# Causal attention on one core: row maxima of heads 1 to 7 sent through DRAM, and the maxima's mask added by a matmul

## The chip, the cores and the metric

The kernel runs on one core of a Trainium2 chip. A core has five engines that run their own queues of instructions and wait for each other by semaphores: TensorE (PE; its weight loads are shown apart as PEld), VectorE (DVE), ScalarE (ACT), GpSimd (POOL) and SyncE (SP), which here does nothing but issue DMAs. Matrix products land in PSUM, eight banks of 128 x 512 float32; other tiles lie in SBUF. The metric is the time of one execution on the device, in microseconds (us).

## What is computed

One layer of a decoder trunk: an input projection, an mLSTM branch of 4 heads, an attention branch of 8 heads, an output projection and an MLP. The change lies in the attention:

```python
SEQ, MLA_HEADS, MLA_NOPE, MLA_ROPE, MLA_V = 2048, 8, 64, 32, 64
scale = (MLA_NOPE + MLA_ROPE) ** -0.5
sc = jnp.einsum('bhqd,bkhd->bhqk', q, k) * scale
sc = jnp.where(kpos[None, :] <= qpos[:, None], sc, -jnp.inf)
p = jax.nn.softmax(sc, axis=-1)
h = jnp.einsum('bhqk,bkhd->bqhd', p, v)
```

## The kernel before

The program is a list of small operations, each with an engine, an estimated duration, the operations it needs, a key (a due time) and the buffers of a ring that it takes and frees. `Plan.run` (line 154) simulates the engines with these estimates and lays the operations down in the order that comes out; `pin` (line 255) then holds each engine but SP to that order. So estimates, such as `n / 2.4 + 15` ns for a matmul of `n` columns, decide which instruction stands behind which, and an engine never runs its queue in another order. SP's DMAs stand in the planned order too.

Attention goes head by head (h = 0 to 7) and in each head over four blocks of 512 queries (qb = 0 to 3). For a pair (h, qb) there are two stages:

- *Maxima* (`maxima`, line 1548). For each of four groups j of 128 queries and each block kb <= qb of 512 keys, one matmul (line 1569) makes rough scores in one of three PSUM banks (rings "m" and "q"), and VectorE reduces them to one maximum per query in `mp`. Where kb < qb this is a plain reduction (line 1574). Where kb = qb, the diagonal piece of (j + 1) x 128 columns, a custom instruction adds the causal mask `maskneg` and takes the maximum in one go, followed by a read of the accumulator (line 1576). There are 192 plain and 128 diagonal pieces in all. Then `top_` (line 1595) reduces `mp` to `mx`, 128 partitions by 4; `rows_` (line 1600) turns that into one row of 512 by four matmuls against the identity, into a bank of the same rings, called `mt`; and `put` (line 1603) copies the row, negated, into partition 96 of the query tile `QK`. The key tile has ones there, so the score matmuls subtract each query's maximum on their own.
- *Steps* (`step`, line 1615). For each tile kt of 128 keys, three matmuls of split float32 operands make transposed scores S (lines 245 to 247); on the diagonal a fourth, in bf16, adds the mask (line 1629: `identb` as weights, `maskb` streamed, 128 columns). ScalarE takes the exponential twice (lines 1633 and 1637), VectorE or GpSimd the low part pl (line 1641), and PE multiplies with V (lines 1652 to 1657). At a block's end ScalarE and VectorE take the product out (ot, lines 1724 and 1727; ou, line 1731), SP stores it, and the sums go through DRAM (sumd, rsm, recd; lines 1738 to 1748).

The maxima are planned to run ahead of the steps that need them (`LEAD`, some 25 tiles). A score of (h, qb) needs the row of (h, qb).

Of the kernel before, what the change touches and what calls it, by code (L numbers as in the profile page):

```python
# [22 lines left out]
TB = 512  # L23
# [4 lines left out]
NH = 8  # L28
QSCALE2 = 96.0
NEG = -3.0e38  # L30
# [7 lines left out]
TB_ = 1  # L38
TR_ = 1
EARLY = ()  # L40
EKEY = -165.0
EGAP = 1.5
LOL = 20.0
# [60 lines left out]

C_CONVW, C_CONVB, C_GPRE, C_HN, C_QN, C_KVN, C_N = 0, 16, 20, 28, 32, 34, 35

K_ID, K_MASKT, K_INV, K_OFF, K_NOT, K_C, K_MASK, K_N = 0, 128, 256, 257, 258, 259, 259, 771

R_BG, R_POST, R_PRE, R_POSTM, R_N = 0, 8, 8 + DM, 8 + 2 * DM, 8 + 3 * DM

# [10 lines left out]
def f32(ap):  # L121
    return ap.bitcast(F32)


class Plan:
# [11 lines left out]
    def ring(self, name, bufs, when=None):  # L137

        self.rings[name] = [bufs, [], when]
# [97 lines left out]
def trunk(ctx: ExitStack, tc: tile.TileContext, x, xT, pos, wu, wout, wup, wdn, cols, rows, consts, edge, out, dbg=None):  # L237
# [3 lines left out]
    vec, act, pool, pe = nc.vector, nc.scalar, nc.gpsimd, nc.tensor  # L241
    dma = nc.sync.dma_start
# [6 lines left out]
    def sb(stack, name, bufs, side="left"):  # L249
        return stack.enter_context(tc.tile_pool(name=name, bufs=bufs, side=side, reuse_waits="tile"))  # L250
# [35 lines left out]
    trep = [dram.tile([P, 2, TB], F32, tag=f"trep{b}", name=f"trep{b}") for b in range(NB)]  # L286
    trigd = dram.tile([64, SEQ], F32, tag="trigd", name="trigd")
    sumd = dram.tile([NH, SEQ], F32, tag="sumd", name="sumd")
    recd = dram.tile([NH, SEQ], F32, tag="recd", name="recd")
    x1d = out  # L290
    x1Td = dram.tile([DM, SEQ // 2], F32, tag="x1Td", name="x1Td")
# [4 lines left out]
    pl = Plan()  # L296
# [1107 lines left out]

    V = {}
    pools = {}
    a2 = av = ar2 = pq = pS = po = onecol = maskneg = maskb = identb = None
    pm = []
    QK, Qh, Ql, Kh, Kl = ([None, None] for _ in range(5))

# [5 lines left out]

    def switch1():

        nonlocal a2, maskneg, pq
        s_e.close()  # L1420
        a2 = sb(pc, "a2", 2)
        a1 = sb(pc, "a1", 1)
        set_tiles(a1, 0)
        maskneg = a1.tile([P, 512], F32, tag="maskneg", name="maskneg")
        pq = pp(pc, "pq", 1)

    def switch2():
# [4 lines left out]

    def switch3():

        nonlocal av, ar2, pS, po, maskb, identb, onecol
        s_b.close()
        pools["work0"] = sb(ctx, "work0", 1, "right")
        av = sb(pa, "av", 1, "right")
        maskb = av.tile([P, P], BF16, tag="maskb", name="maskb")
        identb = av.tile([P, P], BF16, tag="identb", name="identb")  # L1440
        act.copy(maskb, maskT)
        act.copy(identb, ident)
# [70 lines left out]
    o_kr, o_k, o_q, o_m, o_sc, o_pv, o_v = {}, {}, {}, {}, {}, {}, {}  # L1513
# [34 lines left out]
    def maxima(h, qb, keys):  # L1548
        s = h % 2
        mp = {}  # L1550
        reds = []

        def ring(i):
            return "q" if (h, qb) in EARLY or i % 3 == 2 else "m"

        def bank(i, name):
            return (pq if ring(i) == "q" else pm[0]).tile([P, TB], F32, tag=ring(i), name=name)

        def piece(j, kb, key):
            n = TB if kb < qb else (j + 1) * P  # L1560
            t = {}
            i = len(reds)

            def mm():
                if "t" not in mp:
                    mp["t"] = a2.tile([P, 4, 4], F32, tag="mp", name=f"mp{h}_{qb}", bufs=4)
                q0 = qb * TB + j * P
                t["p"] = ps = bank(i, f"m{h}_{qb}_{j}_{kb}")
                pe.matmul(ps[:, :n], Qh[s][0:96, q0 : q0 + P], Kh[s][0:96, kb * TB : kb * TB + n], start=True, stop=True)  # L1569

            def red():
                ps = t["p"]
                if kb < qb:
                    vec.tensor_reduce(mp["t"][:, j, kb : kb + 1], ps, axis=AX.X, op=ALU.max)  # L1574
                else:
                    vec.tensor_tensor_reduce(  # L1576
                        out=ps[:, :n], in0=ps[:, :n], in1=maskneg[:, 512 - n :], op0=ALU.add, op1=ALU.max, scale=1.0, scalar=NEG,
                        accum_out=mp["t"][:, j, kb : kb + 1],
                    )

            head = not reds
            a = pl.op("PE", n / 2.4 + (56 if n == P else 15), mm, [o_q[h, qb][0], o_k[h, kb][0], o_kr[s, kb], o_const[s]], key, take=(ring(i), "mp") if head else (ring(i),))
            if head:
                mp["op"] = a
            reds.append(pl.op("DVE", n / 0.96 + (148 if kb < qb else 285), red, [a, o_mask] if head else [a, o_mask, mp["op"]], key - 3, free=[(ring(i), a)]))

        todo = [(j, kb) for j in range(4) for kb in range(qb + 1)]
        for (j, kb), key in zip(todo, keys):
            piece(j, kb, key)
        t = {}  # L1590
        key = keys[-1] - 3

        def top_():
            t["m"] = a2.tile([P, 32], F32R, tag="mx", name=f"mx{h}_{qb}")[:, 0:4]
            vec.tensor_reduce(t["m"], mp["t"][:, :, 0 : qb + 1], axis=AX.X, op=ALU.max)

        def rows_():
            t["p"] = bank(len(reds), f"mt{h}_{qb}")
            for j in range(4):
                pe.matmul(t["p"][0:1, j * P : (j + 1) * P], t["m"][:, j : j + 1], identr, start=True, stop=True)  # L1600

        def put():
            act.activation(Qh[s][96:97, qb * TB : (qb + 1) * TB], t["p"][0:1], AF.Copy, scale=-1.0)
# [3 lines left out]
        war = [o_sc[n] for n, (hh, q, _) in enumerate(blocks) if (hh, q) == (h - 2, qb)]  # L1607
# [195 lines left out]
    n = GT * P  # L1803
# [856 lines left out]
def prepare(inputs):  # L2660
    a = {k: np.asarray(v) for k, v in inputs.items()}
# [24 lines left out]
    def cv(v):  # L2686
# [7 lines left out]
    consts = np.zeros((P, K_N), np.float32)  # L2694
    consts[:, K_ID : K_ID + P] = np.eye(P)
    r = np.arange(P)
    consts[:, K_MASK + 384 : K_MASK + 512] = np.where(r[None, :] <= r[:, None], 0.0, NEG)
    consts[:, K_MASKT : K_MASKT + P] = np.where(r[None, :] >= r[:, None], 0.0, NEG)
# [39 lines left out]
```

## Time and profile before

| | us |
|---|---|
| time before, median of 3 runs | 2419.19 |
| the three runs | 2416.09, 2419.19, 2419.89 |
| the profiled execution, its own time | 2418.22 |
| its span in the profile | 2415.7 |
| PE busy in the span | 2372.5 |
| first matmul of the maxima, start | 516.0 |
| last step of attention on VectorE (line 1641), start | 992.1 |

The span is 2.5 us shorter than the execution's time; what lies around it is start and end. A row of the profile's timeline gives start, duration, engine, line of the kernel, operation, and output<-inputs with their shapes. PE's rows overlap, as a matmul's duration holds its way through the array; the time that one takes from the next is the distance of their starts. In the waits, "PEld S L245 <- DVE pl L1641" says that a weight load for S waited for VectorE's pl.

### The profile page before, as it was taken

Reading aid. Unit: us, or ns where it says so; the run is one execution under the profiler, and the core shown is the slowest. Engines: PE = TensorE matmul, PEld = TensorE weight load, DVE = VectorE, ACT = ScalarE, POOL = GpSimd, SP = SyncE. Lnnn points to the kernel's source line nnn. Section 1 sums busy time; section 2 is a strip of 40 time slices with the busy share of each in tenths; the row PEclk is TensorE's granted clock in tenths of the full one; section 3 lists DMA queues with packets and bytes.
Section 4 is the critical chain, followed back from the end, with each engine's and each line's share of the span. In section 5 each row is a group of like instructions: output and inputs, shape, how many; then the busy total and the mean of one; then the engine's idle time right before and its main releaser. Section 6 shows DMA issues by size and latency. Waiting matters only on the chain.

```text
span 2415.7 us, 34327 instructions
## 1 busy us (share of the span) xinstructions
PE 2372.5 (98%) x11135; PEld 1907.3 (79%) x11135; DVE 1722.8 (71%) x3125; ACT 1363.1 (56%) x2646; POOL 814.0 (34%) x697
## 2 busy tenths in 40 slices
PE   9999999999999999999999999999999999999997
PEld 7787777777777777788888888888888888888885
DVE  6865665658888887646866687766675677676778
ACT  5645454437788777544666556755665343443454
POOL 2634343428888888432000000000000322322346
PEclk9999999989999999999999999999999999999999
DMA  7697979887222321567877697755664435445448
GB/s 280 219 320 229 336 239 337 271 208 168 72 57 54 80 60 26 157 202 249 258 213 227 195 327 225 210 171 166 184 214 144 159 127 183 129 136 169 133 136 167
DMA packets 341308, 449.21 MB, mean 186 GB/s; under 512 B 34908, under 2 KB 227432, under 8 KB 341128
## 3 DMA queue, kind: packets, MB, share of 16 engines
q1 hardware_dynamic: 337192, 440.16, 58.6%
q0 software_dynamic: 3936, 6.87, 2.0%
q8 instruction: 87, 1.43, 0.2%
q14 instruction: 93, 0.76, 0.1%
HBM read 295.97 MB, written 153.05 MB: 186 GB/s over the span
## 4 chain that ended last, share of the span: by engine, by line
PE 53%; DVE 1%; DMA 1%; issue 0%; ACT 0%; SPq 0%; POOL 0%; DVEq 0%; ACTq 0%; POOLq 0%
PE op L245 1%; PE op L246 1%; PE op L247 1%; PE d_4X L2510 1%; PE d_3X L2512 1%; PE d_5X L2512 1%; PE d_4X L2512 1%; PE d_1X L2512 1%; PE d_1X L2511 1%; PE d_2X L2511 1%; PE d_3X L2511 1%; PE d_2X L2512 1%; PE d_4X L2511 1%; PE d_5X L2511 1%; PE d_5X L2510 1%; PE d_1X L2510 1%
## 5 line engine op out<-in xcount | busy, mean ns | idle before, releaser
L2548 POOL TENSOR_TENSOR y<-vd_0X,y 128x512 f32<-128x512 f32 x7 | 10.3, 1475 | 726.1 <-ACT vd_0X L2545 726.1
L1668 POOL TENSOR_TENSOR t<-t,ph 128x512 f32<-128x512 f32 (+1 forms) x192 | 213.0, 1110 | 17.8 <-ACT ph L1633 7.4
L1633 ACT ACTIVATE ph<-S 128x512 fp32r<-128x512 f32 (+1 forms) x320 | 170.4, 533 | 84.2 <-PE S L247 51.7
L2460 ACT CAST hh<-hr 128x512 fp32r<-128x512 f32 (+1 forms) x208 | 116.3, 567 | 156.1 <-DMA hr<-hd 15.3
L1641 DVE TENSOR_TENSOR pl<-S,ph 128x512 fp32r<-128x512 f32 (+3 forms) x272 | 157.1, 589 | 33.1 <-ACT S L1637 30.2
L245 PE MATMUL mm<-xh,wh 128*128 128x512 f32 x384 | 157.2, 409 | 5.4 <-ACT vs L813 1.9
L2465 DVE TENSOR_TENSOR hl<-hr,hh 128x512 fp32r<-128x512 f32 (+1 forms) x208 | 133.0, 647 | 30.2 <-ACT hh L2460 23.9
L246 PE MATMUL mm<-xl,wh 128*128 128x512 f32 x384 | 151.3, 394 | 0.9 <-DVE xl L416 0.9
L247 PE MATMUL mm<-xh,wl 128*128 128x512 f32 x384 | 151.1, 393 | 0.5 <-DVE wl L491 0.5
L1574 DVE TENSOR_REDUCE mp<-m 128x1 f32<-128x512 f32 x192 | 128.7, 681 | 19.1 <-PE m L1569 18.4
L1637 ACT ACTIVATE S<-S 128x512 f32<-128x512 f32 (+3 forms) x272 | 140.8, 518 | 0.4
L245 PE MATMUL S<-QK 97*128 97x512 f32 (+1 forms) x320 | 121.3, 379 | 2.4 <-DVE pl L1641 2.3
L1654 PE MATMUL o<-ph,V 128*128 128x512 f32 (+1 forms) x320 | 118.9, 378 | 2.2 <-DVE ot L1727 1.8
L1569 PE MATMUL m<-QK 96*128 96x512 f32 (+3 forms) x320 | 117.7, 400 | 1.3 <-DVE mp L1576 0.6
L246 PE MATMUL S<-QK 97*128 97x512 f32 (+1 forms) x320 | 118.2, 369 | 0.0
L247 PE MATMUL S<-QK 97*128 97x512 f32 (+1 forms) x320 | 117.8, 368 | 0.0
L1657 PE MATMUL o<-pl,V 128*65 128x512 f32 (+1 forms) x320 | 115.6, 362 | 0.6 <-POOL pl L1641 0.5
L245 PE MATMUL op<-wo,hh 128*128 128x512 f32 x256 | 101.0, 395 | 0.3 <-DVE osm L1958 0.2
L2299 ACT ACTIVATE t<-t 128x512 f32<-128x512 f32 x96 | 60.6, 632 | 70.8 <-DVE t L2294 70.1
L247 PE MATMUL op<-wo,hl 128*128 128x512 f32 x256 | 99.9, 390 | 0.0
L246 PE MATMUL op<-wo,hh 128*128 128x512 f32 x256 | 99.8, 390 | 0.0
L245 PEld LDWEIGHTS mm<-xh,wh 128*128 128x128 f32 x384 | 72.5, 189 | 26.9 <-ACT vs L813 2.4
(6451 smaller groups left out, 7485.9 us busy)
## 6 DMA issues: line engine op xcount, KB each, us to landing
hr<-hd SPq DMA_DIRECT2D x100, 448.0 KB
wr<-in_wu_dram SPq DMA_DIRECT2D x71, 512.0 KB
hd<-t SPq DMA_DIRECT2D x128, 256.0 KB
hd<-ts SPq DMA_DIRECT2D x96, 256.0 KB
wl<-wparts SPq DMA_DIRECT2D x45, 512.0 KB
QK<-qkd SPq DMA_DIRECT2D x32, 512.0 KB
xt<-in_x_dram SPq DMA_DIRECT2D x28, 512.0 KB
xf<-xd SPq DMA_DIRECT2D x40, 256.0 KB
```

The source lines that it names most:

```text
L245: pe.matmul(o, ah, bh, start=start, stop=False)
L246: pe.matmul(o, ah, bl, start=False, stop=False)
L247: pe.matmul(o, al, bh, start=False, stop=stop)
L1574: vec.tensor_reduce(mp["t"][:, j, kb : kb + 1], ps, axis=AX.X, op=ALU.max)
L1633: act.activation(t["h"][:, :w], t["S"][:, :w], AF.Exp)
L1637: act.activation(t["p"][:, :w], t["S"][:, :w], AF.Exp)
L1641: (pool if by_pool else vec).tensor_tensor(t["l"][:, :w], t["p"][:, :w], f32(t["h"][:, :w]), ALU.subtract)
L1654: pe.matmul(o0, v[:, 0:128], t["h"][:, :w], start=start, stop=stop)
L1668: pool.tensor_tensor(to, to, hv, ALU.add)
L2465: vec.tensor_tensor(t["l", m][:, :w], t["r", m][:, :w], f32(t["h", m][:, :w]), ALU.subtract)
L2511: pe.matmul(ps, a, w[:, 1], start=False, stop=False, skip_group_check=True)
L2512: pe.matmul(ps, b, w[:, 0], start=False, stop=stop, skip_group_check=True)
```

## The change

1. Diagonal pieces of the maxima: a bf16 matmul of 128 columns adds the mask in PSUM (weights `maskb`, streamed `identb`), and VectorE makes a plain reduction of n columns. The custom instruction, the accumulator read and the tile `maskneg` with its load are gone.
2. For heads 1 to 7 (`MROW = 1`), `rows_` and `put` are gone. SP writes `mx` to DRAM (`lay`, 512 elements of 4 bytes) and reads the row back into partition 96 of `QK` (`fetch`, 2 KB). Head 0 keeps the matmuls and the copy. `mx` has three buffers for two.
3. The sign moves: the key tile has -1 in partition 96, and the row isn't negated.
4. The bf16 mask and identity come ready from the host in the constants; ScalarE's two casts are gone.
5. The planner's estimates follow: 60 ns for the mask matmul, `n / 0.96 + 148` ns for the reduction.

```diff
-    maskT = cst[:, K_MASKT : K_MASKT + P]
+    maskb, identb = (cst[:, K_MASKT + i : K_MASKT + i + P // 2].bitcast(BF16) for i in (0, P // 2))
...
-        ("mp", 4, o_s1), ("mx", 2, o_s1), ("rsm", 2, o_s3),
+        ("mp", 4, o_s1), ("mx", 3, o_s1), ("rsm", 2, o_s3),
...
-    o_mask = pl.op("SP", 500, lambda: dma(maskneg, consts[:, K_MASK : K_MASK + 512]), [o_s1], key=EKEY - 30, kb=256)
...
-                pe.matmul(ps[:, :n], Qh[s][0:96, q0 : q0 + P], Kh[s][0:96, kb * TB : kb * TB + n], start=True, stop=True)
+                pe.matmul(ps[:, :n], Qh[s][0:96, q0 : q0 + P], Kh[s][0:96, kb * TB : kb * TB + n], start=True, stop=kb < qb)
+                if kb == qb:
+                    pe.matmul(ps[:, n - P : n], maskb, identb, start=False, stop=True)
...
-                ps = t["p"]
-                if kb < qb:
-                    vec.tensor_reduce(mp["t"][:, j, kb : kb + 1], ps, axis=AX.X, op=ALU.max)
-                else:
-                    vec.tensor_tensor_reduce(
-                        out=ps[:, :n], in0=ps[:, :n], in1=maskneg[:, 512 - n :], op0=ALU.add, op1=ALU.max, scale=1.0, scalar=NEG,
-                        accum_out=mp["t"][:, j, kb : kb + 1],
-                    )
+                vec.tensor_reduce(mp["t"][:, j, kb : kb + 1], t["p"][:, :n], axis=AX.X, op=ALU.max)
...
-            act.activation(Qh[s][96:97, qb * TB : (qb + 1) * TB], t["p"][0:1], AF.Copy, scale=-1.0)
+            act.activation(Qh[s][96:97, qb * TB : (qb + 1) * TB], t["p"][0:1], AF.Copy)
+
+        def lay():
+            dma(mrowd[h, qb * TB : (qb + 1) * TB].rearrange("(j p) -> p j", p=P), f32(t["m"]))
+
+        def fetch():
+            dma(f32(Qh[s][96:97, qb * TB : (qb + 1) * TB]), mrowd[h : h + 1, qb * TB : (qb + 1) * TB])
...
+        if h >= MROW:
+            b = pl.op("SP", 500, lay, [a], key, free=[("mx", a)], kb=128)
+            o_m[h, qb] = pl.op("SP", 500, fetch, [b] + war, key, kb=64)
+            return
...
-        "edge": np.stack([np.ones(SEQ, np.float32), np.zeros(SEQ, np.float32)]),
+        "edge": np.stack([-np.ones(SEQ, np.float32), np.zeros(SEQ, np.float32)]),
```

Lines of the changed kernel are numbered a little otherwise: 1565 for the maxima's matmul, 1567 for its mask, 1570 for the reduction, 1597 for `lay`, 1600 for `fetch`, 246 to 248 for the three matmuls.

The orders of the two programs agree but for attention. Three places are shown; a name such as m_1_0_1 is a piece of qb 1, j 0, kb 1.

PE in the first part, head 0, before the first scores. Before:

```order
L1600 MATMUL mt_0_5143<-identr,mx_0_5137 1x128 x4
L1569 MATMUL m_1_0_1_5149<-QK_4840 128x128
L1569 MATMUL m_1_1_1_5156<-QK_4840 128x256
L1569 MATMUL m_1_2_0_5165<-QK_4840 128x512
L1569 MATMUL m_1_2_1_5168<-QK_4840 128x384
L1569 MATMUL m_1_3_0_5171<-QK_4840 128x512
```

And now:

```order
L1591 MATMUL mt_0_5145<-identr,mx_0_5140 1x128 x4
L1565 MATMUL m_1_0_1_5151<-QK_4841 128x128
L1567 LDWEIGHTS cst
L1567 MATMUL m_1_0_1_5151<-cst 128x128
L1565 MATMUL m_1_2_1_5157<-QK_4841 128x384
L1567 LDWEIGHTS cst
L1567 MATMUL m_1_2_1_5157<-cst 128x128
L1565 MATMUL m_1_1_1_5161<-QK_4841 128x256
L1567 LDWEIGHTS cst
L1567 MATMUL m_1_1_1_5161<-cst 128x128
L1565 MATMUL m_1_2_0_5174<-QK_4841 128x512
```

Each diagonal piece is followed by its mask, a weight load and a matmul of 128 columns, and the diagonal pieces have moved ahead of the wide ones. The set mt stays, as this is head 0.

PE in the steady part, head 4, block 2 of the steps, where the row of block 3 is made. Before:

```order
L247 MATMUL S_2_5_8621<-QK_4840 128x512
L1600 MATMUL mt_3_8629<-identr,mx_3_8617 1x128 x4
L1654 MATMUL o_4_2_8585<-ph_2_11_8576,V_5246 128x128
L1657 MATMUL o_4_2_8586<-pl_2_11_8594,V_5246 65x128
L1569 MATMUL m_0_3_0_8641<-QK_5248 128x512
```

And now:

```order
L248 MATMUL S_2_5_8640<-QK_4841 128x512
L1565 MATMUL m_0_1_0_8652<-QK_5257 128x256
L1567 LDWEIGHTS cst
L1567 MATMUL m_0_1_0_8652<-cst 128x128
L1565 MATMUL m_0_3_0_8655<-QK_5257 128x512
L1567 LDWEIGHTS cst
L1567 MATMUL m_0_3_0_8655<-cst 128x128
L1655 MATMUL o_4_2_8602<-ph_2_11_8591,V_5255 128x128
L1658 MATMUL o_4_2_8603<-pl_2_11_8610,V_5255 65x128
```

The set mt is gone from its place, and two masks of the next head's maxima stand there.

SP at the same place. Before:

```order
L1738 DMA sumd<-ou_1_8563 1x512
L1748 DMA recd<-rsm_0_8533 128x4
L1737 DMA hT<-ot_1_8560 64x512
L1742 DMA rsm_1_8664<-sumd 128x4
L1748 DMA recd<-rsm_1_8664 128x4
```

And now:

```order
L1739 DMA sumd<-ou_1_8584 1x512
L1749 DMA recd<-rsm_0_8545 128x4
L1738 DMA hT<-ot_1_8572 64x512
L1743 DMA rsm_1_8681<-sumd 128x4
L1597 DMA mrowd<-mx_3_8645 128x4x1
L1600 DMA QK_4841<-mrowd 1x512
L1597 DMA mrowd<-mx_0_8700 128x4x1
L1600 DMA QK_5257<-mrowd 1x512
L1749 DMA recd<-rsm_1_8681 128x4
```

Two lays and two fetches stand between the load and the store of rsm_1, behind the store of ot_1.

More of the change, by code (lines that the diff above doesn't have):

```diff
@@ L40 @@
 EARLY = ()
+MROW = 1
 EKEY = -165.0
@@ L1406, in trunk @@
     pools = {}
-    a2 = av = ar2 = pq = pS = po = onecol = maskneg = maskb = identb = None
+    a2 = av = ar2 = pq = pS = po = onecol = None
     pm = []
@@ L1417, in switch1 @@
     def switch1():
-        nonlocal a2, maskneg, pq
+        nonlocal a2, pq
         s_e.close()
@@ L1423, in switch1 @@
         set_tiles(a1, 0)
-        maskneg = a1.tile([P, 512], F32, tag="maskneg", name="maskneg")
         pq = pp(pc, "pq", 1)
@@ L1433, in switch3 @@
     def switch3():
-        nonlocal av, ar2, pS, po, maskb, identb, onecol
+        nonlocal av, ar2, pS, po, onecol
         s_b.close()
@@ L1438, in switch3 @@
         av = sb(pa, "av", 1, "right")
[L1439 to L1442, printed above, removed]
         ar2 = sb(pa, "ar2", 2, "right")
@@ L1568, in mm @@
                 t["p"] = ps = bank(i, f"m{h}_{qb}_{j}_{kb}")
-                pe.matmul(ps[:, :n], Qh[s][0:96, q0 : q0 + P], Kh[s][0:96, kb * TB : kb * TB + n], start=True, stop=True)
+                pe.matmul(ps[:, :n], Qh[s][0:96, q0 : q0 + P], Kh[s][0:96, kb * TB : kb * TB + n], start=True, stop=kb < qb)
+                if kb == qb:
+                    pe.matmul(ps[:, n - P : n], maskb, identb, start=False, stop=True)
             def red():
-                ps = t["p"]
-                if kb < qb:
-                    vec.tensor_reduce(mp["t"][:, j, kb : kb + 1], ps, axis=AX.X, op=ALU.max)
-                else:
-                    vec.tensor_tensor_reduce(
-                        out=ps[:, :n], in0=ps[:, :n], in1=maskneg[:, 512 - n :], op0=ALU.add, op1=ALU.max, scale=1.0, scalar=NEG,
-                        accum_out=mp["t"][:, j, kb : kb + 1],
-                    )
+                vec.tensor_reduce(mp["t"][:, j, kb : kb + 1], t["p"][:, :n], axis=AX.X, op=ALU.max)
             head = not reds
-            a = pl.op("PE", n / 2.4 + (56 if n == P else 15), mm, [o_q[h, qb][0], o_k[h, kb][0], o_kr[s, kb], o_const[s]], key, take=(ring(i), "mp") if head else (ring(i),))
+            a = pl.op("PE", n / 2.4 + (56 if n == P else 15) + (60 if kb == qb else 0), mm, [o_q[h, qb][0], o_k[h, kb][0], o_kr[s, kb], o_const[s]], key, take=(ring(i), "mp") if head else (ring(i),))
             if head:
                 mp["op"] = a
-            reds.append(pl.op("DVE", n / 0.96 + (148 if kb < qb else 285), red, [a, o_mask] if head else [a, o_mask, mp["op"]], key - 3, free=[(ring(i), a)]))
+            reds.append(pl.op("DVE", n / 0.96 + 148, red, [a] if head else [a, mp["op"]], key - 3, free=[(ring(i), a)]))
         todo = [(j, kb) for j in range(4) for kb in range(qb + 1)]
@@ L1602, in put @@
         def put():
-            act.activation(Qh[s][96:97, qb * TB : (qb + 1) * TB], t["p"][0:1], AF.Copy, scale=-1.0)
-        a = pl.op("DVE", 80, top_, reds, key, take=("mx",), free=[("mp", mp["op"])])
+            act.activation(Qh[s][96:97, qb * TB : (qb + 1) * TB], t["p"][0:1], AF.Copy)
[3 more added lines that the diff above has]
+            dma(f32(Qh[s][96:97, qb * TB : (qb + 1) * TB]), mrowd[h : h + 1, qb * TB : (qb + 1) * TB])
+        a = pl.op("DVE", 80, top_, reds, key, take=("mx",), free=[("mp", mp["op"])])
+        war = [o_sc[n] for n, (hh, q, _) in enumerate(blocks) if (hh, q) == (h - 2, qb)]
+        if h >= MROW:
+            b = pl.op("SP", 500, lay, [a], key, free=[("mx", a)], kb=128)
+            o_m[h, qb] = pl.op("SP", 500, fetch, [b] + war, key, kb=64)
+            return
         b = pl.op("PE", 4 * 75, rows_, [a, o_const[s]], key, take=(ring(len(reds)),), free=[("mx", a)])
-        war = [o_sc[n] for n, (hh, q, _) in enumerate(blocks) if (hh, q) == (h - 2, qb)]
         o_m[h, qb] = pl.op("Activation", 585, put, [b] + war, key, free=[(ring(len(reds)), b)])
@@ L2693, in prepare @@
     rows = np.concatenate([a["b_gates"][0], a["norm_post_mix"][0], a["norm_pre_mlp"][0], a["norm_post_mlp"][0]])[None]
-    consts = np.zeros((P, K_N), np.float32)
+    consts = np.zeros((P, K_C), np.float32)
     consts[:, K_ID : K_ID + P] = np.eye(P)
     r = np.arange(P)
-    consts[:, K_MASK + 384 : K_MASK + 512] = np.where(r[None, :] <= r[:, None], 0.0, NEG)
-    consts[:, K_MASKT : K_MASKT + P] = np.where(r[None, :] >= r[:, None], 0.0, NEG)
+    halves = np.concatenate([np.where(r[None, :] >= r[:, None], 0.0, NEG), np.eye(P)], axis=1).astype(np.float32)
+    consts[:, K_MASKT : K_MASKT + P] = np.ascontiguousarray((halves.view(np.uint32) >> 16).astype(np.uint16)).view(np.float32)
     inv = np.array(INV_FREQ_BITS, np.uint32).view(np.float32)
```

5 lines of the change are left out of this document (3 added, 2 removed).

## Prediction

> **What bounds the kernel now.** I read the page first: the engines' busy time and the chain that ended last.
>
> ```profile
> PE 2372.5 (98%) x11135; PEld 1907.3 (79%) x11135; DVE 1722.8 (71%) x3125; ACT 1363.1 (56%) x2646; POOL 814.0 (34%) x697
> PE 53%; DVE 1%; DMA 1%; issue 0%; ACT 0%; SPq 0%; POOL 0%; DVEq 0%; ACTq 0%; POOLq 0%
> ```
>
> TensorE (PE) is busy for 98% of the span, and of the chain's attributed share nearly all is PE. So a slot added to or taken from PE counts in full, unless it stands in a stretch where PE waits. The change touches attention alone, so next I cut that stretch, and two moments of the projections, into windows. The columns are: stretch, length, then busy time (instructions) of PE, PEld (its weight loads), VectorE (DVE), ScalarE (ACT) and GpSimd (POOL), then the granted PE clock, the DMA engines' share and GB/s.
>
> ```profile
> 111.91:115.33 3.42, 1.23 (x4) 0.75 (x5) 2.65 (x3) 3.42 (x6) 2.90 (x4) 1.00 0.29 117
> 115.33:118.74 3.41, 3.41 (x9) 2.64 (x9) 3.41 (x4) 2.63 (x5) 3.33 (x2) 0.50 0.89 306
> 446.42:449.83 3.41, 1.88 (x7) 0.97 (x6) 2.21 (x4) 3.36 (x9) 1.88 (x2) 1.00 0.30 104
> 521.51:524.93 3.42, 2.49 (x12) 1.20 (x10) 3.24 (x15) 2.06 (x9) 0.13 (x1) 1.00 1.06 269
> 524.93:531.20 6.27, 5.82 (x16) 3.56 (x17) 5.98 (x17) 1.08 (x3) 2.71 (x7) 0.50 0.55 147
> 531.20:542.00 10.80, 10.80 (x33) 8.17 (x32) 5.83 (x17) 4.15 (x10) 1.26 (x1) 0.50 1.08 219
> 545.00:990.00 445.00, 438.69 (x2250) 335.80 (x2249) 376.94 (x821) 349.42 (x729) 369.19 (x316) 1.00 0.32 75
> ```
>
> Attention has two parts. From 516 to 531 us only the maxima of head 0 and the last mLSTM work run: VectorE is the busy one (5.98 of 6.27 us) and PE has holes. After one thin window (2.49 of 3.42 us busy) the granted clock falls to half for 17 us; from 531.2 to 542 PE is full, at half clock. From 545 to 990 PE is busy 438.69 of 445 us, while the other three have about a fifth or less to spare. I call that the steady part. Third come the waits of the weight loads there (engine, line waited for, total us, times, longest):
>
> ```profile
> PEld S L245 <- DVE pl L1641: 5.4, 9, 1.2
> PEld o L1680 <- POOL tl L1676: 3.0, 6, 1.1
> PEld o L1654 <- DVE ot L1727: 1.9, 5, 0.6
> ```
>
> What PE still waits for is VectorE (7.3 us) and GpSimd (3.0 us).
>
> **The sum, part by part.** First, the slots on PE. The mask matmul that the change adds to the maxima already exists in the scores (L1629), and the matmuls it removes are L1600:
>
> ```profile
> 791.98 0.41 PE L1600 MATMUL mt<-identr,mx 128*1 128x128 f32 x4
> 792.22 0.45 PE L1654 MATMUL o<-ph,V 128*128 128x512 f32 x1
> 792.51 0.40 PE L1657 MATMUL o<-pl,V 128*65 128x512 f32 x1
> 792.75 0.28 PE L1569 MATMUL m<-QK 96*128 96x256 f32 x1
> ...
> 793.57 0.23 PE L1629 MATMUL S<-maskb,identb 128*128 128x128 bf16 x1
> 793.61 0.48 PE L1654 MATMUL o<-ph,V 128*128 128x512 f32 x1
> 793.93 0.40 PE L1657 MATMUL o<-pl,V 128*65 128x512 f32 x1
> 794.17 0.39 PE L1569 MATMUL m<-QK 96*128 96x512 f32 x1
> 794.40 0.39 PE L245 MATMUL S<-QK 97*128 97x512 f32 x1
> ```
>
> Durations are no price here, since matmuls overlap; starts are. A 512-column matmul goes every 0.23 us (794.17 to 794.40). The mask takes 0.04 us from its start to the next, but that next one then takes 0.32 (793.61 to 793.93), 0.09 more than normal; I read that as its weight load, which no longer fits behind so short a matmul. The price of a mask is 0.13 us. Four row matmuls take 0.24 us and lengthen their follower to 0.29, by 0.06: 0.30 us a set.
>
> ```profile
> L1629 PE MATMUL S<-maskb,identb 128*128 128x128 bf16 x128 | 30.1, 235 | 0.0
> L1600 PE MATMUL mt<-identr,mx 128*1 128x128 f32 x128 | 13.2, 226 | 0.1
> ```
>
> There are 128 diagonal pieces, as in the scores, and 32 sets, of which head 0 keeps 4. Masks: 96 pieces of 256 to 512 columns at 0.13 is 12.5 us. For the 32 pieces of 128 columns I take 0.07, between 0.04 and 0.13, because the short piece already left the next load bare: 2.2 us (1.3 to 4.2). Sets removed: 28 x 0.30 = 8.4 us. PE gains **+6.3 us** of slots (5.4 to 8.3).
>
> Some of this lies beside other work. Before the first scores some 9 masks stand where PE waits for VectorE, so about 1.2 us is hidden: **-1.2**. If that cover went, it would be paid.
>
> Second, VectorE. A diagonal piece was a custom maximum and an accumulator read, and becomes a plain reduction:
>
> ```profile
> 525.05 0.14 DVE L1576 DVE_READ_ACCUMULATOR2_ANT mp<- 128x1 f32 x1
> 525.05 0.69 DVE L1574 TENSOR_REDUCE mp<-m 128x1 f32<-128x512 f32 x1
> 525.65 0.69 DVE L1576 CUSTOM_DVE_ANT_0 m<-m,maskneg 128x512 f32<-128x512 f32 x1
> 526.26 0.14 DVE L1576 DVE_READ_ACCUMULATOR2_ANT mp<- 128x1 f32 x1
> 526.26 0.75 DVE L1274 TENSOR_TENSOR hn<-num,sm 128x256 f32<-128x256 f32 x2
> ```
>
> By starts both big forms take 0.60 us, and the read has no start of its own before the next. The relief lies between 0 and the read's 0.14 us; I take 0.05, near the starts: 6.4 us over 128 pieces (0 to 18). In the first part, bound by VectorE, 9 pieces give **-0.5**.
>
> Third, ScalarE loses the copy of a row into QK:
>
> ```profile
> L1603 ACT ACTIVATE QK<-mt 1x512 fp32r<-1x512 f32 x32 | 18.7, 585 | 13.3 <-PE mt L1600 6.5 <-DMA V<-vd 6.0
> ```
>
> That is 28 x 0.585 = 16.4 us of its queue. ScalarE and VectorE make the pl and ot that PE waits for, 7.3 us in the steady part. Relief of a few per cent cannot remove all of it; I take a third, **-2.5** (0 to -7.3, and a gain lost to a worse order is possible). The PSUM bank that a set held until the copy is free too; no wait in the steady part names it, so 0.
>
> Fourth, the clock. The window 521.51 to 524.93 lost it with 2.49 us busy. Busy time does not sort the windows: 1.88 us with 7 wide matmuls kept it, 1.23 us with 4 wide ones lost it. The 12 of ours were mostly narrow. In the new order masks stand behind m_1_0_1, m_1_2_1, m_1_1_1 and m_2_0_2, about there: four loads and 512 streamed columns more. I expect this window to come out above the mark. Then 531.2 to 542, 10.8 us of full PE at half clock, takes half as long: **-5.4**. The stretch before it is VectorE's and gains nothing.
>
> [...]
>
> Nothing: the removed load of maskneg and the two casts, which no wait names, and the changed constants.
>
> Sum: 6.3 - 1.2 - 0.5 - 2.5 - 5.4 = -3.3 us. The profiled execution took 2418.22 us, so 2414.9, say **2415**. The median of the runs shown is 2419.19, 1.0 above that execution, so this is 0.17% under the median. About 0.2%, 4.8 us, is what a measurement of this kernel tells from no change.
>
> **The new wait.** For heads 1 to 7 the row now goes to DRAM and back, both on SP's queue, where the fetch waits for the lay, and everything behind it on SP with it: stores of ot, the sumd and recd round trips, loads of QK and wor. Who waits then is ScalarE for ot's buffer and VectorE for rsm. The tight blocks are the last of each head, (h, 3); here that of head 4:
>
> ```profile
> 785.93 0.15 DVE L1595 TENSOR_REDUCE mx<-mp 128x4 fp32r<-128x16 f32 x1
> 788.38 0.59 ACT L1603 ACTIVATE QK<-mt 1x512 fp32r<-1x512 f32 x1
> ```
>
> The nearest DMAs are the round trip of the sums, first and last starts by line and then two issues of one block:
>
> ```profile
> L1738 SPq DMA_DIRECT2D sumd<-ou x32: 235/242/434, 554.7 to 997.6; - x32
> L1742 SPq DMA_DIRECT2D rsm<-sumd x32: 325/530/1312, 557.8 to 1006.8; - x32
> L1745 DVE RECIPROCAL rsm<-rsm x32: 154/166/179, 562.1 to 1009.1; 128x4 f32<-128x4 f32 x32
> 713.09 0.39 SPq L1738 DMA_DIRECT2D sumd<-ou  x1
> 714.85 0.53 SPq L1742 DMA_DIRECT2D rsm<-sumd  x1
> ```
>
> mx is done at 786.08, and by the program's order the first score of that block is the one at 794.40 above: 8.3 us, of which the copy of the row took until 788.97. Counting slots in the two orders between such a block's last maximum and its first score, the new one has 0.2 us more here, and from 1.1 less (head 6) to 4.1 more (head 7). A small write is readable 1.8 us after its issue (713.09 to 714.85), and a read of 128 pieces reaches its reader within 4.3 us (557.8 to 562.1). So the two steps take 3.5 to 8.6 us; I take 5, nearer the write, and it is hidden. If it is not, see below.
>
> [...]
>
> **The rivals.**
> - The clock falls all the same (in this trace or because its windows lie otherwise). Then the sum is +2.1: 2420. For it: 1.23 and 2.49 us busy both lost it. Against: four more masks.
> - Attention is held more by latency than by slots. Then freeing ScalarE's 16.4 us and a PSUM bank removes all 7.3 us, the clock stays, and the sum is -8.1: 2410. For it: three engines at 78 to 85% in the steady part. Against: PE's idle time there is 6.3 us in all.
> - **Slower:** the row comes late. Place: the first score of blocks (h, 3), and the SP queue behind the fetch. It decides from the point where lay plus fetch take over 8.3 us from mx, for which SP being held by another wait is enough. Seven blocks at 1.5 to 3 us each would be 10 to 21 us, so 2425 to 2436. Against: no score ever waited for a row before.
> - The change does not do what it says: the masks cost 0.23 us (their duration) rather than 0.13. Then 128 x 0.10 = 12.8 us more: 2428. The starts speak plainly against it.
>
> **How the numbers follow.** Forecast 0.43, clock falls 0.28, latency 0.15, late row 0.11, dear masks 0.03. The forecast's own bounds (slots 5.4 to 8.3, relief 0 to 7.3) give 2409 to 2420. The range 2408 to 2425 takes in the first two rivals and leaves out the bulk of the last two and the far ends. Faster by over 0.2% (under 2414.4): half of the forecast's and most of the latency case, 0.37. Slower (over 2424): late row, dear masks and an end of the clock case, 0.16. Within: 0.47.
>
> **What will show it.** PE busy between first maximum and last score some 6 us more in slots; starts around each new mask 0.13 us longer; clock 1.00 from 525 to 542 (0.50 is the first rival); waits of S on pl and of o on ot smaller by a third; no wait of S on the fetch, and none of ACT on the store of ot. A wait of S on the row, or SP's rows of ot and rsm later by more than 2 us, would make the prediction wrong.

## The result: 2.6% slower, and the profile after

The changed kernel took 2479.7 us (median of 4 runs, 2477.88 to 2486.83) against 2418.77 for the kernel before; the ratio is 1.0259, with a 95% interval of 1.0236 to 1.0282. The prediction, 2415 us in a range of 2408 to 2425, was wrong by its sign and by 65 us. The profiled execution took 2478.14 us, with a span of 2476.3.

The busy time of the engines and the chain that ended last, from the page of the changed kernel:

```profile
PE 2394.7 (97%) x11151; PEld 1914.0 (77%) x11151; DVE 1716.5 (69%) x2997; ACT 1347.3 (54%) x2616; POOL 814.7 (33%) x697
PE 83%; DMA 8%; DVE 4%; issue 1%; ACT 1%; SPq 1%; POOL 1%; DVEq 0%; POOLq 0%; ACTq 0%
```

DMA has 8% of this chain, some 200 us in which the chain ran through transfers. In e8 below, the same kernel with a quick store, the chain also covers the whole span and DMA has 3%. The chain before, with 1%, can't be set against them: it is followed back only to 1057 us, so its shares add up to some 55%, and no part of attention is in it. The windows of the changed kernel, with the columns of the prediction's, show where PE lost time:

```profile
524.93:531.20 6.27, 5.30 (x19) 3.48 (x19) 5.54 (x12) 0.58 (x1) 1.90 (x7) 0.56 0.44 119
531.20:542.00 10.80, 10.80 (x42) 7.84 (x42) 6.13 (x13) 4.99 (x12) 1.27 (x1) 0.62 1.07 222
545.00:990.00 445.00, 407.29 (x2016) 303.02 (x2014) 327.88 (x638) 295.06 (x615) 324.24 (x280) 0.95 0.36 66
```

In the steady part PE is busy 407.29 us where it was 438.69, 31.4 us less, and the granted clock is 0.95 where it was 1.00: an estimated 22 us of work more lost in 445. From the first matmul of the maxima to the last step's pl on VectorE, attention takes 534.5 us (514.4 to 1048.9) for 476.1 (516.0 to 992.1). That is 58.4 of the 60.6 us by which the span grew, so nearly all of the loss is in attention.

Waits between 515 and 1060 us of the changed kernel, those on transfers and on pl (engine, line waited for, total us, times, longest):

```profile
DVE rsm L1746 <- DMA rsm<-sumd: 37.4, 10, 9.0
PEld S L246 <- DVE pl L1642: 26.0, 11, 8.1
PE S L246 <- DVE pl L1642: 23.0, 8, 7.7
PE S L246 <- DMA QK<-mrowd: 8.5, 2, 4.5
ACT ot L1725 <- DMA hT<-ot: 6.6, 4, 3.4
```

The score is shown waiting for its own row only twice, 8.5 us in all. The largest wait on a transfer is on another one: VectorE stands 37.4 us for rsm, the sums that come back from DRAM for the reciprocal, and PE then stands for VectorE's pl (weight loads 5.4 us before, 26.0 now). One such place, from the timeline of the changed kernel (start, duration, engine, line, operation; SP's rows are issues), SP first, then VectorE, then PE:

```profile
648.51 0.54 SPq L1597 DMA_DIRECT2D mrowd<-mx  x1
649.16 0.58 SPq L1743 DMA_DIRECT2D rsm<-sumd  x1
658.56 0.24 SPq L1600 DMA_DIRECT2D QK<-mrowd  x1
659.21 0.55 SPq L1519 DMA_DIRECT2D QK<-qkd  x1
...
649.72 0.68 DVE L1570 TENSOR_REDUCE mp<-m 128x1 f32<-128x512 f32 x1
658.73 0.18 DVE L1746 RECIPROCAL rsm<-rsm 128x4 f32<-128x4 f32 x1 [8.32 <-DMA rsm<-sumd]
658.82 0.66 DVE L1642 TENSOR_TENSOR pl<-S,ph 128x512 fp32r<-128x512 f32 x1
...
659.54 0.79 PE L246 MATMUL S<-QK 97*128 97x512 f32 x1 [6.96 <-DVE pl L1642]
```

The store of the maxima (lay) is issued at 648.51, and SP, which waits for it, issues the fetch at 658.56: 10.1 us. Over all 28 stores this distance is 8.1 to 10.9 us, 9.7 in the mean. The read of rsm, issued 0.6 us behind the store, comes 9.6 us later as well, at the same moment as the store. Behind it VectorE stands 8.32 us and PE 6.96. All ten waits for rsm are of this kind: in seven the read of rsm was issued between a store of the maxima and its fetch, and in the other three the store of the sums (sumd) that the read has to wait for. The DMA view of the same kernel for 653 to 658.7 us (busy share and GB/s in 40 slices, then packets) shows what moves meanwhile:

```profile
DMA  0000000000000000000000000000000000000000
DMA packets 0, 0.00 MB, mean 0 GB/s; under 512 B 0, under 2 KB 0, under 8 KB 0
```

Nothing. All packets have left before 653 us, those of the read of rsm too, and still that read ends only at 658.70 us, 9.54 after its issue. The chain of waits of the changed kernel has that read, and a store that is one piece of the same 2 KB (sumd) close to a store of the maxima (start, us, what):

```profile
649.16 9.54 DMA rsm<-sumd
...
686.02 10.78 DMA mrowd<-mx
697.20 1.84 DMA sumd<-ou
```

2 KB as 512 pieces of 4 bytes take 10.78 us, 2 KB as one piece 1.84.

### The profile page after: what moved, and what is told of

Same layout as the page of the kernel before. It is cut to its first block, busy times and chain, and to the rows that moved or that the text cites. A ratio compares the mean times of both kernels' runs of the same rounds, so it can differ in the third digit from the quotient of the medians.

```text
span 2476.3 us, 34307 instructions
## 1 busy us (share of the span) xinstructions
PE 2394.7 (97%) x11151; PEld 1914.0 (77%) x11151; DVE 1716.5 (69%) x2997; ACT 1347.3 (54%) x2616; POOL 814.7 (33%) x697
## 4 chain that ended last, share of the span: by engine, by line
PE 83%; DMA 8%; DVE 4%; issue 1%; ACT 1%; SPq 1%; POOL 1%; DVEq 0%; POOLq 0%; ACTq 0%
PE mm L246 3%; PE mm L247 3%; PE mm L248 3%; PE op L246 2%; PE op L247 2%; PE op L248 2%; PE S L246 2%; PE o L1655 2%; DMA rsm<-sumd 2%; PE m L1565 2%; PE o L1658 2%; PE S L247 2%; PE S L248 2%; DMA mrowd<-mx 2%; PE mv L246 1%
## 5 line engine op out<-in xcount | busy, mean ns | idle before, releaser
L1570 DVE TENSOR_REDUCE mp<-m 128x1 f32<-128x512 f32 (+2 forms) x320 | 186.2, 601 | 57.2 <-PE m L1565 30.1
L246 PE MATMUL S<-QK 97*128 97x512 f32 (+1 forms) x320 | 129.9, 406 | 31.5 <-DVE pl L1642 23.0
L1565 PE MATMUL m<-QK 96*128 96x512 f32 (+2 forms) x320 | 123.9, 407 | 4.1 <-DVE mp L1570 3.1
L247 PE MATMUL S<-QK 97*128 97x512 f32 (+1 forms) x320 | 120.1, 375 | 0.0
L248 PE MATMUL S<-QK 97*128 97x512 f32 (+1 forms) x320 | 119.9, 375 | 0.0
L246 PEld LDWEIGHTS S<-QK 97*128 97x128 f32 x320 | 64.1, 200 | 48.1 <-DVE pl L1642 26.0
```

The costliest lines, as they stand in the source:

```text
L246: pe.matmul(o, ah, bh, start=start, stop=False)
L247: pe.matmul(o, ah, bl, start=False, stop=False)
L248: pe.matmul(o, al, bh, start=False, stop=stop)
L1570: vec.tensor_reduce(mp["t"][:, j, kb : kb + 1], t["p"][:, :n], axis=AX.X, op=ALU.max)
```

## The experiments

Theory S: the store of 512 pieces of 4 bytes completes some 9.7 us after its issue, and it holds up SP and the transfers behind it. Rivals: M, the masks on PE and the clock; Q, the place of the added DMAs in SP's order; R, pieces of 4 bytes are slow wherever they go. The table has every run; the store-to-fetch time is the mean distance of the two issues in SP's timeline, the stretch runs from the first matmul of the maxima to the last pl, and the last column is the total of "DVE rsm <- DMA rsm<-sumd" between 515 and 1060 us. Ratios are to the kernel before, measured beside each run (2416.86 to 2418.77 us). The last three columns are read from one profiled execution of each kernel, whose time lies up to 5.3 us from the kernel's median (e9); differences of a few us in the attention column say little.

| run | median us | ratio, 95% interval | store to fetch us | attention us | wait for rsm us |
|---|---|---|---|---|---|
| before | 2418.77 | | | 476.1 | 0.7 |
| changed kernel | 2479.70 | 1.0259 (1.0236 to 1.0282) | 9.7 | 534.5 | 37.4 |
| e1, masks alone | 2429.14 | 1.0044 (1.0029 to 1.0059) | | 485.6 | 1.3 |
| e2, rows alone | 2488.58 | 1.0290 (1.0274 to 1.0306) | 10.2 | 541.9 | 45.5 |
| e3, pieces of 16 bytes | 2426.09 | 1.0031 (1.0021 to 1.0040) | 3.9 | 478.6 | 2.9 |
| e4, within SBUF | 2419.16 | 1.0005 (0.9995 to 1.0015) | | 475.5 | 0.4 |
| e5, planner told | 2479.43 | 1.0255 (1.0241 to 1.0269) | 9.9 | 538.9 | 47.4 |
| e6, store by ScalarE | 2482.51 | 1.0272 (1.0257 to 1.0288) | 9.6 | 534.2 | 42.6 |
| e8, 64 bytes apart | 2424.35 | 1.0028 (1.0017 to 1.0040) | 3.4 | 479.3 | 3.6 |
| e10, 32 bytes apart | 2424.45 | 1.0033 (1.0020 to 1.0045) | 3.5 | 478.8 | 3.8 |
| e9, 16 bytes apart | 2426.67 | 1.0033 (1.0022 to 1.0044) | 4.0 | 478.9 | 4.8 |
| e11, 8 bytes apart | 2424.49 | 1.0032 (1.0020 to 1.0044) | 5.1 | 480.5 | 7.1 |
| e7, before with rows in SBUF | 2412.98 | 0.9982 (0.9973 to 0.9991) | | 468.6 | 2.0 |
| e12, before with rows 64 apart | 2413.38 | 0.9978 (0.9969 to 0.9987) | 4.1 | 471.5 | 0.7 |

### The two parts apart (e1, e2)

The masks alone, with the rows as before:

```diff
-MROW = 1
+MROW = 8
```

> All eight heads make their rows on PE again (MROW = 8); the mask matmul and the plain reduction stay. Theory S (the scattered store is the cause: it lands some 9.5 us after its issue and holds SP and the DMA queue behind it): the 61 us are nearly all gone. PE pays its slots, 14.7 us less 1.7 us hidden, with some relief of VectorE, so 2424 to 2433 us. Rival M (the masks on PE, and the halved clock that follows, are the cause): 2465 us or more.

Ratio 1.0044: 11 us slower, where the whole change costs over 60. Rival M is out as the main cause. The second run has the rows through DRAM alone, VectorE's maximum with the mask kept:

```diff
         def put():
-            act.activation(Qh[s][96:97, qb * TB : (qb + 1) * TB], t["p"][0:1], AF.Copy, scale=-1.0)
+            act.activation(Qh[s][96:97, qb * TB : (qb + 1) * TB], t["p"][0:1], AF.Copy)
...
+        def lay():
+            dma(mrowd[h, qb * TB : (qb + 1) * TB].rearrange("(j p) -> p j", p=P), f32(t["m"]))
...
+        def fetch():
+            dma(f32(Qh[s][96:97, qb * TB : (qb + 1) * TB]), mrowd[h : h + 1, qb * TB : (qb + 1) * TB])
...
```

> The kernel before, with its custom maximum and maskneg, and only the rows of heads 1 to 7 through DRAM. Theory S: the new wait is all here, so 2455 to 2472 us: some 55 us of holes, less 8.4 us of slots that the row matmuls no longer take; VectorE waits for rsm some 30 to 40 us in all. Rival M: 2408 to 2414 us, the slots saved and nothing else.

2488.58 us: the rows carry the loss, and alone they cost at least about as much as the whole change (1.0290 for 1.0259; the intervals just overlap). That was a miss in size (2455 to 2472 expected). Its waits are larger, 45.5 us on rsm in 14 places and 19.2 on the row (37.4 in 10 and 8.5 in the changed kernel). Why this order collides more often isn't settled.

### Which property of the store (e3, e4)

In e3 the four maxima of a query go out as one piece of 16 bytes, and the fetch puts them in order:

```diff
-            dma(mrowd[h, qb * TB : (qb + 1) * TB].rearrange("(j p) -> p j", p=P), f32(t["m"]))
+            dma(mrowd[h, qb * TB : (qb + 1) * TB].rearrange("(p j) -> p j", p=P), f32(t["m"]))
...
-            dma(f32(Qh[s][96:97, qb * TB : (qb + 1) * TB]), mrowd[h : h + 1, qb * TB : (qb + 1) * TB])
+            row = mrowd[h : h + 1, qb * TB : (qb + 1) * TB].rearrange("o (p j) -> o j p", p=P)
+            dma(f32(Qh[s][96:97, qb * TB : (qb + 1) * TB]).rearrange("o (j p) -> o j p", p=P), row)
```

> As the change, but the store writes 128 pieces of 16 bytes, in the order in which mx lies, and the fetch puts them in order while reading (512 elements of 4 bytes). Theory S: it is the pieces of the store to DRAM that cost, so the time from store to fetch falls from 9.7 to 4 us or less, and the kernel takes 2414 to 2430 us. Rival Q (two more DMAs per block in SP's planned order are the cause, whatever their pieces): still 9 us and 2470 us or more. Rival R (small pieces cost in either direction): the store is quick but the fetch lands 9 us late, and scores wait for the row, over 2440 us.

Two DMAs at the same two places, and 2426.09 us. Store to fetch falls to 3.9 us, the wait for rsm to 2.9. Rival Q is out: the number of DMAs and their order are the same. In e4 the pieces of 4 bytes stay, but go from SBUF to SBUF:

```diff
-            dma(mrowd[h, qb * TB : (qb + 1) * TB].rearrange("(j p) -> p j", p=P), f32(t["m"]))
+            for j in range(4):
+                dma(f32(Qh[s][96:97, qb * TB + j * P : qb * TB + (j + 1) * P]), f32(t["m"][:, j : j + 1]))
```

> As the change, but without DRAM: four DMAs of 128 elements of 4 bytes from mx straight into the row. The pieces are as small and as many, only the target is SBUF. Theory S in the form that the store to DRAM is what is slow: 2410 to 2424 us, VectorE hardly waits for rsm. If pieces of 4 bytes are slow to any target: 2450 us or more, with scores waiting for the row.

2419.16 us, no different from the kernel before, with the same 512 pieces a block. Rival R is out: pieces of 4 bytes are not slow wherever they go.

### Who is held: SP, its queue, or all (e5, e6)

In e5 the planner counts 9.5 us for the store:

```diff
+    SLOW = 9500.0
...
+            if d in self.slow:
+                return end[d] + self.SLOW
             return end[d] + (self.DMA if ops[d][0] == "SP" else self.HOP)
...
             b = pl.op("SP", 500, lay, [a], key, free=[("mx", a)], kb=128)
+            pl.slow.add(b)
```

> The changed kernel, with the planner told that the store of the maxima takes 9.5 us more before the row can be fetched (it took it for 1.9); the store, the fetch and the masks are unchanged. Theory S in two parts. S1, SyncE stands at the fetch until the store has landed, and what is behind it in SyncE's order comes late: the fetch now stands later in that order, SyncE no longer stands there, and the time falls to 2420 to 2438 us. S2, the transfers that are issued right behind a store land only with it, whoever waits where: the order helps little, and the time stays at 2455 to 2480 us. If the cost were the longer way of the row alone, with no place in which it could be hidden: 2470 to 2490 us.

2479.43 us, no gain. From its timeline, SP and then VectorE:

```profile
582.61 0.55 SPq L1601 DMA_DIRECT2D mrowd<-mx  x1
583.72 0.34 SPq L1748 DMA_DIRECT2D rsm<-sumd  x1
584.10 2.60 SPq L1538 DMA_DIRECT2D V<-vd  x2
593.49 0.24 SPq L1604 DMA_DIRECT2D QK<-mrowd  x1
...
593.76 0.18 DVE L1751 RECIPROCAL rsm<-rsm 128x4 f32<-128x4 f32 x1 [7.78 <-DMA rsm<-sumd]
```

SP now has two loads of V to issue between store and fetch, but it still stands from 586.70 to 593.49, and rsm is still late by as much. The new order did not free SP altogether, so S1 alone isn't refuted by this run; that rsm was issued in time and still came late speaks for S2. In seven of the ten longest waits for rsm here it is the store of the sums, not the read, that was issued between a store of the maxima and its fetch: the new order moved the collision. The time would also fit the third case, the longer way of the row alone, but no wait of a score on the fetch shows between 515 and 1060 us, against 47.4 us on rsm.

In e6 ScalarE issues the store, into a queue of its own; the store counts 1.9 us for the planner.

```diff
-            dma(mrowd[h, qb * TB : (qb + 1) * TB].rearrange("(j p) -> p j", p=P), f32(t["m"]))
+            nc.scalar.dma_start(mrowd[h, qb * TB : (qb + 1) * TB].rearrange("(j p) -> p j", p=P), f32(t["m"]))
...
-            b = pl.op("SP", 500, lay, [a], key, free=[("mx", a)], kb=128)
+            b = pl.op("Activation", 60, lay, [a], key, free=[("mx", a)], kb=128)
+            pl.slow.add(b)
...
```

> The changed kernel, with the store issued by ScalarE into a DMA queue of its own, and the planner's figure for the store at 1.9 us as in the changed kernel; the fetch stays on SyncE. S1 (SyncE stands at the fetch): SyncE still stands there some 8 us a block, 2455 to 2485 us. S2 (transfers behind a store on its queue land with it): the reads of the reciprocals are on another queue than the store and no longer late, VectorE's waits for them go from 37 us to below 10, and the time falls to 2425 to 2450 us. If the hold is not of the queue but of the DMA engines or of the memory, the waits for the reciprocals stay and the time too.

2482.51 us. Its timeline, ScalarE's issue of the store, then SP, then VectorE:

```profile
629.76 0.37 ACTq L1601 DMA_DIRECT2D mrowd<-mx  x1
...
630.60 0.54 SPq L1748 DMA_DIRECT2D rsm<-sumd  x1
631.19 0.43 SPq L1872 DMA_DIRECT2D wor<-in_wout_dram  x1
641.06 0.24 SPq L1604 DMA_DIRECT2D QK<-mrowd  x1
...
641.68 0.18 DVE L1751 RECIPROCAL rsm<-rsm 128x4 f32<-128x4 f32 x1 [7.43 <-DMA rsm<-sumd]
```

The read of rsm is on SP's queue (q1 in the profile), the store on ScalarE's (q10), and rsm still lands with the store, 11.1 us after its issue. The waits for rsm stay, 42.6 us: the hold isn't of the queue, so S2 fell in that form. SP still stands at the fetch here, until 641.06, and the time lies in the range of S1; but the read of rsm was issued before that stand, so S1 doesn't explain why it is late. The DMA view of this run for 634 to 641 us (queue: packets, MB, share of 16 engines) shows the load of weights, wor, that was issued at 631.19:

```profile
q1 hardware_dynamic: 75, 0.27, 52.1%
```

0.27 MB held the engines for 52.1% of 16 x 7 us, 58 us of their time. In the next 2 us, 641 to 643, with the store landed, the same queue shows:

```profile
q1 hardware_dynamic: 106, 0.26, 40.8%
```

That is 0.26 MB for 40.8% of 16 x 2 us, 13 us. Byte for byte, loads from DRAM here took more than four times as long while the store completed. So the hold lies in something that both queues share, such as the DMA engines or the memory; the runs don't tell which.

### The spacing (e8 to e11)

The same 512 pieces of 4 bytes, at the same places in the program, but spread in DRAM:

```diff
-    mrowd = dram.tile([NH, SEQ], F32, tag="mrowd", name="mrowd")
+    mrowd = dram.tile([NH, SEQ, 16], F32, tag="mrowd", name="mrowd")
...
-            dma(mrowd[h, qb * TB : (qb + 1) * TB].rearrange("(j p) -> p j", p=P), f32(t["m"]))
+            dma(mrowd[h, qb * TB : (qb + 1) * TB, 0].rearrange("(j p) -> p j", p=P), f32(t["m"]))
...
-            dma(f32(Qh[s][96:97, qb * TB : (qb + 1) * TB]), mrowd[h : h + 1, qb * TB : (qb + 1) * TB])
+            dma(f32(Qh[s][96:97, qb * TB : (qb + 1) * TB]), mrowd[h : h + 1, qb * TB : (qb + 1) * TB, 0])
```

> The changed kernel, with the 512 elements of 4 bytes of each store laid 64 bytes apart in DRAM, and the fetch reading them from there. If the store is late because neighbouring 4-byte pieces are written into the same few lines of memory, it now lands in some 2 to 4 us as a store of whole rows does, and the time falls to 2418 to 2435 us. If it is late because of the number of small pieces alone (512 against the 128 of 16 bytes in the third run), it lands as late as before, the fetch of 512 scattered pieces takes longer besides, and the time is 2470 to 2510 us.

2424.35 us; store to fetch 3.4 us. From its timeline, SP and VectorE:

```profile
667.30 0.39 SPq L1597 DMA_DIRECT2D mrowd<-mx  x1
668.20 0.32 SPq L1743 DMA_DIRECT2D rsm<-sumd  x1
670.29 0.52 SPq L1600 DMA_DIRECT2D QK<-mrowd  x1
...
675.27 0.17 DVE L1746 RECIPROCAL rsm<-rsm 128x4 f32<-128x4 f32 x1
```

The fetch follows after 3.0 us, and VectorE shows no idle time before the reciprocal. Only the addresses differ from the changed kernel, and with them the fetch, which now reads 512 pieces; 55 us are gone. The spacing was then varied, the 16 of the diff being 4 (e9), 8 (e10) and 2 (e11):

> As the run with the pieces 64 bytes apart, but 16 bytes apart, 512 pieces of 4 bytes as there. Theory S as it now stands: what is slow is many 4-byte writes into the same few lines of memory, and everything that is to end behind them waits, on whichever queue. With a quarter of the pieces to each stretch of memory the store-to-fetch time goes from 9.7 us (4 apart) towards that of 64 apart (3.3 us): 4 to 6 us if it goes by pieces per stretch, and the time of the kernel to 2425 to 2450 us. If only pieces that touch (4 apart) are slow, it is 3.3 us already, and 2422 to 2428 us. If 64 bytes are the unit, and two pieces in one are as bad as sixteen: 9 to 10 us and 2470 us or more.

> The same with the pieces 32 bytes apart. By pieces per stretch: a store-to-fetch time of 3.3 to 4.5 us and 2422 to 2432 us. If two pieces in one unit of 64 bytes are as bad as sixteen: 9 to 10 us and 2470 us or more.

> As the runs at 16, 32 and 64 bytes apart, but 8 bytes. Store to fetch took 9.7 us in the mean at 4 bytes apart, 4.0 at 16, 3.5 at 32 and 3.4 at 64. If the wait grows with the pieces that share a stretch of memory: 5 to 7 us, and 2428 to 2455 us. If it is only pieces without a gap between them that are slow: 3.5 to 4.5 us, and 2422 to 2430 us. If 8 apart is as bad as 4: over 9 us and 2465 us or more.

Store to fetch in the mean: 9.7 us at 4 bytes apart, 5.1 at 8, 4.0 at 16, 3.5 at 32, 3.4 at 64; the shortest of the 28 are 8.1, 3.3, 2.6, 1.9 and 1.8. So it grows as the pieces come closer, and most steeply at the end. In the kernel's time the four spaced runs can't be told apart (1.0028 to 1.0033): up to 5 us are hidden, 9.7 are not. The expectation for e11 had the store to fetch right (5 to 7 us), not the kernel's time (2428 to 2455 us).

### What the change would be worth with a good store (e7, e12)

In e7 the kernel before, with VectorE's maximum and mask, gets its rows by the four transfers within SBUF of e4; in e12 by the two of e8 (the diffs are those of e2 with the lines of e4 and of e8).

> The kernel before, with the rows of heads 1 to 7 moved by four transfers of 128 pieces of 4 bytes within SBUF in place of TensorE's transposes and ScalarE's copies; its VectorE maximum with the mask is kept, and there is no masking matmul. Theory: the 28 sets of transposes leave TensorE (28 by 0.30, 8.4 us) and nothing comes in their place, 2408 to 2415 us, faster than both kernels. Rival: VectorE and SyncE, not TensorE, hold the steady part in this form, so that the freed slots become waits: 2416 to 2424 us.

> The kernel before, with the rows of heads 1 to 7 through DRAM at 64 bytes a piece, its VectorE maximum with the mask kept: the change without its masking matmuls and without its slow store. Theory: the masking matmuls cost what they save (the first run, and the runs with a good store at 1.003 of before), and the transposes' 8.4 us of TensorE are the whole gain: 2410 to 2416 us, like the run with the rows within SBUF (2413.0). Rival: two transfers one after the other are later than four at once and the row holds the scores up: 2417 to 2425 us.

2412.98 and 2413.38 us, ratios 0.9982 and 0.9978: these are the fastest kernels of the study, and both forecasts by the theory held. They gain some 4 to 5 us of the 8.4 by which the transposes were priced. In e7 the attention stretch shortens by 7.5, but the rest of the span grows by 1.9. One of the waits that stayed, in e12 between 515 and 1060 us:

```profile
PEld S L246 <- DVE pl L1653: 7.5, 14, 1.2
PE S L246 <- DVE pl L1653: 2.5, 7, 0.8
```

For the weight loads that was 5.4 us before: PE, with less to do, waits a little more for VectorE.

## Why the prediction was wrong, step by step

**The new wait: the step that failed.** The prediction put it so: "the two steps take 3.5 to 8.6 us; I take 5, nearer the write, and it is hidden". The bounds were built from a store of one piece of 2 KB (1.8 us) and from a read of 128 pieces. The store of 512 neighbouring pieces of 4 bytes took 9.7 us in the mean (8.1 to 10.9) by itself, more than the upper bound for both steps together, so the bounds did not bound: neither row had small *writes*, many of them, next to each other in DRAM. Two transfers that share the size with the new one, not the shape, carried the step. The first sentences of that paragraph named the right victims, "everything behind it on SP" and "VectorE for rsm", but the sum priced the wait at nothing. The prediction's own sign of being wrong did come: waits of S on the row, and of ACT on the store of ot (6.6 us).

**The rival "Slower"** had the right kind of mechanism, and the wrong price. It named two places, the first score of blocks (h, 3) and the SP queue behind the fetch, but priced only the first, seven blocks at 1.5 to 3 us. The scores waited 8.5 us for rows. The loss came through rsm, which was in flight beside a store, or whose sums were, in 10 places with up to 9.0 us, and through the clock: by the windows, 31.4 us of PE's busy time and a mean clock of 0.95. In the changed kernel half clock lasted 47.8 us of attention after 545 us, in seven spans; with the store spread (e8) there is none. In the 3.4 us before two of the seven falls PE did nothing, and before the other five it was busy for 0.61 to 1.37 us.

**The clock, -5.4: failed.** "I expect this window to come out above the mark." With the masks in it, in e8, whose order of the masks is the same but whose store is quick:

```profile
521.51:524.93 3.42, 3.03 (x15) 1.69 (x12) 3.38 (x11) 2.06 (x9) 0.00 (x0) 1.00 1.20 294
524.93:531.20 6.27, 5.21 (x17) 3.21 (x16) 5.45 (x14) 0.58 (x1) 2.85 (x7) 0.50 0.22 60
531.20:542.00 10.80, 10.80 (x34) 7.70 (x33) 6.82 (x14) 3.06 (x8) 1.27 (x1) 0.50 1.06 200
```

The window did get busier, 3.03 us for 2.49, and the clock fell behind it all the same, for as long as before. In the changed kernel the clock in the last two of these windows was 0.56 and 0.62. It fell about there, at 524.5 to 527.9 us, in the traces of all fourteen kernels, for 13.7 or 17.1 us. A busier window was not enough, and the first rival (2420 without the 5.4 us) was the better forecast for that part. No window ahead of it was idle: in the 3.4 us up to the fall PE was busy for 2.49 us before, 2.25 in the changed kernel and 3.02 in e8. What sets the clock stays open.

**PE's slots, +6.3, less 1.2 and 0.5.** About right with the rows through DRAM. The price of a mask held; in e1, for one:

```profile
702.35 0.23 PE L1567 MATMUL m<-cst 128*128 128x128 bf16 x1
702.39 0.48 PE L246 MATMUL S<-QK 97*128 97x512 f32 x1
702.71 0.39 PE L247 MATMUL S<-QK 97*128 97x512 f32 x1
```

By starts the mask takes 0.04 us and its follower 0.32 for 0.23. With a good store (e8 to e11, e3) attention took 478.6 to 480.5 us for 476.1, so 2.5 to 4.4 more; the steps gave 4.6 before the relief. With the rows within SBUF (e4), and the same slots, it took 475.5; that the slots don't explain. That PE bounds attention rested on its busy time alone: the chain from which the prediction read PE's share is the one that reaches back only to 1057 us. Taken apart: masks alone +9.5 in the stretch where the masks' terms gave 13.0 before any relief of VectorE, and rows alone (e12, e7) -4.6 and -7.5, where the sets were priced at -8.4. In time the three are +11 us, -5 and -4 by their ratios.

**The relief, -2.5.** The waits of PE's weight loads for pl did fall, from 5.4 to 2.6 us in e8. In the length of attention it doesn't show: 4.6 less 2.5 is 2.1, below all five runs with a good store through DRAM. The runs don't separate it from the errors of the other terms.

**The rest.** The sum without clock and row, 2418.22 + 6.3 - 1.2 - 0.5 - 2.5 = 2420.3, stands against 2424.35 measured in e8. The change as forecast, with a store that completes in time, is thus 0.3% slower (1.0017 to 1.0040), not faster; with the rows within SBUF (e4) it is neither (0.9995 to 1.0015). In the profile of e8, 3.9 of the 7.1 us by which its span is longer lie outside attention. Three spans of half clock that the profile before doesn't have stand there (at 450, 1016 and 2399 us); the 9.6 us of PE's busy time in them would take about half as long at full clock (in the kernel before, the matmuls of 512 columns that start at 531.25 and 531.68 us, at half clock, lie 0.43 us apart; at full clock it is 0.23), so they cost an estimated 4.5 to 4.8 us.

## What to carry to other kernels

In these runs a small DMA couldn't be priced by its bytes, nor by the nearest DMA of the same size; what counted was whether its small pieces were written next to each other in DRAM (512 pieces of 4 bytes took 9.7 us there, and 3.4 us with 64 bytes from one to the next). So before a scattered store of single elements goes into a loop, time one, and lay its pieces apart (e8), join them (e3), or keep them in SBUF (e4). And the slow completion was paid by what else was in flight (37.4 us of waits for rsm, 8.5 for the rows themselves), so look for the tightest reader of any transfer near it, not only for the reader of its own data. A bound taken from rows of another shape is not a bound.

## What the runs showed of the hardware that was not expected

- 512 writes of 4 bytes that lie next to each other in DRAM complete 8.1 to 10.9 us after their issue, though in the place shown the last packet had left within 4.5 us (648.51 to 653). With 64 bytes from one to the next they are done, fetch issued, in 3.4 us (shortest 1.8), and 128 pieces of 16 bytes, gapless, in 3.9.
- While such a store completed, other transfers waited too, on another queue as well: reads of rsm issued 0.6 to 1.1 us behind it in the places shown ended with it, and in e6 loads held the engines 58 us for 0.27 MB, against 13 us for 0.26 MB just afterwards.
- In the changed kernel and in e8 the store is 512 pieces of 4 bytes, and store to fetch takes 9.7 and 3.4 us: what decided here is where they lie. In e10 each piece has 32 bytes of DRAM to itself, and the store is quick (3.5 us); so a write of 4 bytes isn't slow by itself, but many next to each other are. How the memory handles them can't be seen in a trace.
- Not tried: a store that is both planned for 9.5 us and issued from ScalarE.
